# Elementwise work of the mixers moved from GpSimd to VectorE in a two-layer hybrid trunk

## The chip, the cores and the metric

One core of a Trainium2 chip runs the whole program. The metric is device time in microseconds (us): three runs of the kernel before gave 1460.66 to 1461.21 us, median 1460.79 us. The engines are called by the names of the profile: PE (TensorE, matmuls), PEld (its weight loads), DVE (VectorE), ACT (ScalarE), POOL (GpSimd) and SP (SyncE, which only issues DMAs here).

## What is computed

Two layers over 256 tokens of width 1024, all in float32. Each layer is a gated feed-forward block, a mixer of three branches, and a second feed-forward block. The change touches branch a and the rotation of branch c:

```python
u = causal_depthwise_conv(rg_x, conv_w[l], conv_b[l])            # 4 taps
y_a = rg_lru(u, ...) * jax.nn.gelu(rg_g)

def rg_lru(u, w_a, b_a, w_x, b_x, lam):
    r = sigmoid(block_matmul(u, w_a) + b_a)
    i = sigmoid(block_matmul(u, w_x) + b_x)
    log_a = (-RG_C * softplus(-lam)) * r
    a = exp(log_a)
    b = sqrt(-expm1(2.0 * log_a)) * (i * u)
    _, h = associative_scan(combine, (a, b), axis=1)             # h = a*h + b
    return h

def apply_rope(x, cos, sin):
    x1, x2 = split(x, 2, axis=-1)
    return concatenate([x1 * cos - x2 * sin, x2 * cos + x1 * sin], axis=-1)
```

Branch b is a stick-breaking attention, branch c a softmax attention with low-rank queries and keys. The three branches are gated by sigmoids, summed, multiplied by an output matrix and added to x.

## The kernel before

**Matmuls.** float32 values are split in two parts, hi and lo, and a product is made from three of them (hi·hi, hi·lo, lo·hi), so that PE runs at its rate for the fp32r type. The weights come from HBM as one long stream (`raw`, 1 MB a load, issued by SP) and are split on the way in `split_to` (line 414): ACT writes `hi` (a cast of 128x1024), DVE writes `lo` (raw minus hi, 128x1024). Such a 128x1024 stretch is called a piece here. There are 4 buffers each of hi and lo, and the split is made two pieces ahead of the matmul that reads it (`AHEAD`, line 381). A piece feeds 16 matmuls: in `feature_group` (line 511), 8 of 512 columns and 8 of 256.

**Side work.** Everything else is "side work": taking a finished group out of the PSUM banks (`acc`), scaling it, the convolution, the recurrence, the attentions. It is written as Python generators. When the program is built, `Tasks` (line 222) feeds their operations into the stream of matmuls: it keeps a clock for each engine (`Clock`, line 124) that is advanced by fixed costs (`Op`, lines 170 to 190; for DVE 68 + 1.042 ns a column, for POOL 150 + 2.1 ns a column), and `fits` (line 266) lets an operation in when those clocks say that its inputs are there. A small matmul of the side work, which writes a `side` bank, goes in when its inputs will be ready within 60 ns of PE's clock; other work when it starts not later than about 50 ns after that engine's or PE's clock and ends within `LIMIT` (line 227), 1800 ns ahead of PE. The order that comes out is fixed in the program: each engine works through its own list, and waits at an instruction whose inputs are late.

**What the change touches.** `rg_x` (832, with `conv` at 833): u is made of one multiply-add with the bias (line 847, on POOL) and three `scalar_tensor_tensor` on DVE, for each half of 256 columns; its weights `rgw` come by a DMA that POOL issues. `rg_g` (860): gelu by tanh, with the cubic (lines 865 and 866) on POOL. `rg_chain` (879): splits u and its weights in `r` tiles by ACT and DVE, six small matmuls a half into `side`, sigmoids, then the products of lines 910, 925 and 934 on POOL and two scans on DVE. `q_rope` (1062): the rotation of two token tiles (line 1073), one on POOL and one on DVE, six operations each in `rope` (1048). Names in the trace: `f` is any scratch tile of 128x512, `r` a tile of split parts, `rc` the row norms of the two low-rank inputs, `cs` the table of cosines and sines. Nearly every instruction is recorded by one helper and so carries line 201; groups are told apart by their tiles.

What stays on POOL: the sums of squares in `squares` (650), the inverse square roots, one memset in `k_rope`, the `rgw` DMAs, and the last normalisation.

Of the kernel before, what the change touches and what calls it, by code (L numbers as in the profile page):

```python
# [10 lines left out]
AF = mybir.ActivationFunctionType  # L11
ALU = mybir.AluOpType
# [12 lines left out]
V_F1, V_MIX, V_F2, V_CW, V_CB, V_BA, V_BX, V_LAM, V_QN, V_KVN = 0, 8, 16, 24, 56, 64, 72, 80, 88, 90  # L25
# [312 lines left out]
def trunk(tc, xT_in, pos_in, w_in, rgw_in, fin_in, const_in, out):  # L338
# [4 lines left out]
    with ctx:  # L343
# [8 lines left out]
        vec = cst[:, 0:C_FIRST]  # L352
# [19 lines left out]
        act, dve, pe, gp, sp = (  # L372
            Timed(e, n, clock, tasks)
            for e, n in ((nc.scalar, "act"), (nc.vector, "dve"), (nc.tensor, "pe"), (nc.gpsimd, "pool"), (nc.sync, "sp"))
        )
# [456 lines left out]
        def rg_x(mx, p):  # L832
            def conv(f):
                vo = mx["v"]
                w = yield from FT.take()
                gp.dma_start(out=w, in_=rgw_in[mx["l"], :, p * 512:(p + 1) * 512])
                mx["rgw"][p] = w
                u = yield from FT.take()
                for j in range(2):
                    k = p * 2 + j  # L840
                    fs, us = f[:, j * 256:(j + 1) * 256], u[:, j * 256:(j + 1) * 256]

                    def cw(tap):
                        c = vo + V_CW + tap * 8 + k
                        return vec[:, c:c + 1]

                    gp.tensor_scalar(us, fs, cw(3), vec[:, vo + V_CB + k:vo + V_CB + k + 1], op0=ALU.mult, op1=ALU.add)
                    for d in range(1, 4):
                        dve.scalar_tensor_tensor(out=us[:, d:], in0=fs[:, :256 - d], scalar=cw(3 - d), in1=us[:, d:], op0=ALU.mult, op1=ALU.add)
                yield  # L850
                FT.give(f)
                mx["u"][p] = u

            def run(a):
                f = yield from scaled(a, mx["nm"], "rb")
                yield
                tasks.spawn(conv(f))
            return run

        def rg_g(mx, p):  # L860
            def gelu(x):

                t = yield from FT.take()
                act.activation(out=t, in_=x, func=AF.Square)
                gp.tensor_scalar(t, t, 0.044715, 1.0, op0=ALU.mult, op1=ALU.add)
                gp.tensor_tensor(t, t, x, op=ALU.mult)
                act.activation(out=t, in_=t, func=AF.Tanh, scale=0.7978845608028654)
                dve.scalar_tensor_tensor(out=x, in0=t, scalar=1.0, in1=x, op0=ALU.add, op1=ALU.mult)
                yield
                FT.give(t)  # L870
                mx["gT"][p] = x

            def run(a):
                f = yield from scaled(a, mx["nm"], "rb")
                yield
                tasks.spawn(gelu(f))
            return run

        def rg_chain(mx, ps):

            vo = mx["v"]

            for p in ps:
                while p not in mx["u"]:
                    yield 1
                u = mx["u"][p]
                w = mx["rgw"][p]
                wt = yield from RT.take()
                ut = yield from RT.take()
                wr, ur = [x.rearrange("p k c t -> p k (c t)") for x in (wt, ut)]  # L890
                for x, r in ((w, wr), (u, ur)):
                    act.copy(r[:, 0], x)
                    dve.tensor_tensor(r[:, 1], x, r[:, 0].bitcast(F32), op=ALU.subtract)
                A = yield from FT.take()
                I = yield from FT.take()
                T = yield from FT.take()
                for j in range(2):
                    k = 2 * p + j
                    s = slice(j * 256, (j + 1) * 256)
                    b = yield from side.take()  # L900
                    for q in range(2):
                        c = slice((j * 2 + q) * 128, (j * 2 + q + 1) * 128)
                        for x, (i, d) in enumerate(((0, 0), (0, 1), (1, 0))):
                            pe.matmul(b[:, q * 256:(q + 1) * 256], wr[:, i, c], ur[:, d, s], start=x == q == 0, stop=x == 2, skip_group_check=True)
                    for q, (dst, vb) in enumerate(((A, V_BA), (I, V_BX))):
                        act.activation(out=dst[:, s], in_=b[:, q * 256:(q + 1) * 256], func=AF.Sigmoid, bias=vec[:, vo + vb + k:vo + vb + k + 1])
                    yield
                    side.give(b)
                    act.activation(out=T[:, s], in_=A[:, s], func=AF.Tanh, scale=s4[:, mx["l"], k:k + 1], bias=tiny)
                gp.tensor_tensor(I, I, u, op=ALU.mult)  # L910
                yield
                FT.give(w, u)
                RT.give(wt, ut)
                mx["rgw"].pop(p)
                mx["u"].pop(p)
                mx["tanh"] += 1
                while mx["tanh"] < p // 2 * 2 + 2:
                    yield 1
                for j in range(2):
                    s = slice(j * 256, (j + 1) * 256)  # L920
                    act.activation(out=A[:, s], in_=A[:, s], func=AF.Exp, scale=m8[:, mx["l"], 2 * p + j:2 * p + j + 1])
                act.activation(out=T, in_=T, func=AF.Ln)
                act.activation(out=T, in_=T, func=AF.Exp, scale=0.5)
                dve.scalar_tensor_tensor(out=I, in0=A, scalar=1.0, in1=I, op0=ALU.add, op1=ALU.mult)
                gp.tensor_tensor(I, I, T, op=ALU.mult)
                for j in range(2):
                    s = slice(j * 256, (j + 1) * 256)
                    dve.tensor_tensor_scan(T[:, s], A[:, s], I[:, s], 0.0, op0=ALU.mult, op1=ALU.add)
                yield
                FT.give(A, I)  # L930
                while p not in mx["gT"]:
                    yield 1
                g = mx["gT"].pop(p)
                gp.tensor_tensor(g, g, T, op=ALU.mult)
                hl = yield from RT.take()
                hilo(g, hl, g=0.5)
                yield
                FT.give(g, T)
                mx["ya"][p] = hl
# [108 lines left out]
        def rope(e, dst, src, tmp, nh, t):  # L1048

            co = cs[:, 0, t:t + 1].to_broadcast([128, nh, 32])  # L1050
            si = cs[:, 1, t:t + 1].to_broadcast([128, nh, 32])
            e.tensor_tensor(tmp[:, :, 0:32], src[:, :, 32:64], si, op=ALU.mult)
            e.tensor_tensor(tmp[:, :, 32:64], src[:, :, 0:32], si, op=ALU.mult)
            e.tensor_tensor(dst[:, :, 0:32], src[:, :, 0:32], co, op=ALU.mult)
            e.tensor_tensor(dst[:, :, 32:64], src[:, :, 32:64], co, op=ALU.mult)
            e.tensor_tensor(dst[:, :, 0:32], dst[:, :, 0:32], tmp[:, :, 0:32], op=ALU.subtract)
            e.tensor_tensor(dst[:, :, 32:64], dst[:, :, 32:64], tmp[:, :, 32:64], op=ALU.add)

        def split_heads(ap, nh):
            return ap.rearrange("p (h d) -> p h d", h=nh)  # L1060

        def q_rope(mx):
            def run(a):
                qs = yield from gen_scaled(a, mx["rq"])
                yield
                tasks.spawn(rest(qs))

            def rest(qs):
                ro = []
                for t in range(NT):  # L1070
                    f = yield from FT.take()
                    tmp = yield from FT.take()
                    rope((gp, dve)[t], split_heads(f, 8), split_heads(qs[t], 8), split_heads(tmp, 8), 8, t)
                    yield
                    FT.give(tmp)
                    ro.append(f)
                    yield
                FT.give(*qs)
                yield
                for p in range(2):  # L1080
                    b = yield from transpose_pair(ro, p * 256)
                    f = yield from FT.take()
                    act.copy(f, b)
                    yield
                    side.give(b)
                    mx["qr"][p] = f
                FT.give(*ro)
            return run
# [429 lines left out]
```

## Time and profile before

| | us |
|---|---|
| median of 3 runs | 1460.79 |
| the profiled execution | 1463.23 |
| its span, first to last instruction | 1461.4 |
| PE busy | 1442.5 |
| PEld busy | 1261.0 |
| DVE busy | 1108.8 |
| ACT busy | 888.8 |
| POOL busy | 144.5 |

The profiled execution takes 1.8 us more than its span and lies 2.4 us above the median. Mean granted clock of PE: 0.998 of full speed. The mixer of layer 0 runs from about 200 to 552 us of the span, that of layer 1 from about 920 to 1273; the stretches between are the feed-forward blocks. The moved operations stand in the two mixers alone, and alike in both, so what is said of one layer counts twice.

### The profile page before, as it was taken

What the parts mean: (1) busy time and instruction counts of PE and PEld (TensorE: products, weight loads), DVE (VectorE), ACT (ScalarE), POOL (GpSimd) and SP (SyncE); (2) the same over time, 40 slices, a digit from 0 to 9 for tenths busy, and PEclk for the clock granted to TensorE, in tenths of its full rate; (3) what the DMA queues carried; (4) which work ended last, traced back from release to release, by engine and by line L of the source; (5) the groups of instructions that cost most, each with busy time, mean ns of one, the idle gap of its engine ahead of it and who ended that gap; (6) DMA issues with size and microseconds to landing.
All of it is one profiled execution on the core that took longest, in us unless ns stands there. A gap on an engine that the chain in (4) does not pass through costs nothing.

```text
span 1461.4 us, 20833 instructions
## 1 busy us (share of the span) xinstructions
PE 1442.5 (99%) x8276; PEld 1261.0 (86%) x8276; DVE 1108.8 (76%) x1548; ACT 888.8 (61%) x1365; POOL 144.5 (10%) x118
## 2 busy tenths in 40 slices
PE   8999999999999999999999999999999999999998
PEld 7888889888888888888888888898888888888886
DVE  5887567689987788876677776676989877877853
ACT  4665446888665556555455554479885656566543
POOL 2000001123410000000000000111323000100001
PEclk9999999999999999999999999999999999999999
DMA  6555554444543455455545455544444434545452
GB/s 244 201 185 192 200 179 163 170 151 147 197 148 145 171 179 194 179 200 178 198 173 201 177 198 184 200 159 155 141 171 174 173 138 166 199 175 201 176 199 87
DMA packets 37506, 258.17 MB, mean 177 GB/s; under 512 B 4256, under 2 KB 4640, under 8 KB 6816
## 3 DMA queue, kind: packets, MB, share of 16 engines
q1 hardware_dynamic: 35856, 253.16, 48.0%
q0 software_dynamic: 832, 2.62, 0.6%
q8 instruction: 65, 1.06, 0.3%
q10 hardware_dynamic: 720, 1.05, 0.2%
q14 instruction: 33, 0.27, 0.1%
HBM read 255.77 MB, written 1.05 MB: 176 GB/s over the span
## 4 chain that ended last, share of the span: by engine, by line
PE 90%; DVE 7%; issue 1%; ACT 1%; DMA 0%; ACTq 0%; POOLq 0%; POOL 0%; DVEq 0%
PE acc L201 76%; PE side L201 14%; DVE f L201 3%; DVE lo L201 3%; DVE r L201 1%; DMA x<-xT 0%; ACT f L201 0%; ACT hi L201 0%; ACT r L201 0%; ACTq L396 0%; POOLq L1514 0%; POOL rms L201 0%; DVE rms L201 0%; DVEq L201 0%
## 5 line engine op out<-in xcount | busy, mean ns | idle before, releaser
L201 PE MATMUL acc<-r,hi 128*128 128x512 f32 x3116 | 1000.3, 402 | 0.0
L201 DVE TENSOR_TENSOR lo<-raw,hi 128x1024 fp32r<-128x1024 f32 (+1 forms) x478 | 591.4, 1239 | 231.4 <-ACT hi L201 230.2
L201 PEld LDWEIGHTS acc<-r,lo 128*128 128x128 f32 x3116 | 585.2, 188 | 137.7
L201 PE MATMUL acc<-r,lo 128*128 128x256 f32 x3116 | 613.4, 278 | 0.0
L201 ACT CAST hi<-raw 128x1024 fp32r<-128x1024 f32 (+1 forms) x478 | 496.9, 1045 | 128.8 <-PE acc L201 91.9
L201 PEld LDWEIGHTS acc<-r,hi 128*128 128x128 f32 x3116 | 481.5, 189 | 5.0
L201 POOL TENSOR_TENSOR f<-f,f 128x512 f32<-128x512 f32 (+1 forms) x51 | 90.9, 1787 | 1043.3 <-ACT f L201 959.9
L201 ACT COPY f<-acc 128x512 f32<-128x512 f32 x164 | 96.0, 585 | 121.4 <-PE acc L201 121.2
L201 ACT ACTIVATE f<-f 128x256 f32<-128x256 f32 (+3 forms) x190 | 94.9, 502 | 85.6 <-DVE f L201 84.4
L201 DVE TENSOR_TENSOR f<-acc,f 128x512 f32<-128x512 f32 x166 | 113.9, 686 | 41.6 <-ACT f L201 41.2
L201 DVE TENSOR_TENSOR f<-f,f 128x512 f32<-128x512 f32 (+1 forms) x177 | 125.0, 706 | 7.8 <-ACT f L201 1.6
L201 ACT CAST r<-f 128x256 fp32r<-128x256 f32 (+2 forms) x130 | 58.7, 456 | 63.4 <-DVE f L201 59.7
L201 PE MATMUL acc<-hi,r 128*128 128x512 f32 (+2 forms) x344 | 96.9, 358 | 0.0
L201 PE MATMUL side<-r,hi 128*128 128x512 f32 x260 | 84.5, 396 | 0.0
L201 PE MATMUL side<-f,f 128*128 128x256 f32 (+1 forms) x320 | 71.7, 328 | 0.0
L201 PEld LDWEIGHTS acc<-hi,r 128*128 128x128 f32 x344 | 61.6, 189 | 8.3
L201 DVE TENSOR_TENSOR r<-f,r 128x256 fp32r<-128x256 f32 (+2 forms) x130 | 64.7, 502 | 1.9 <-ACT r L201 1.9
L201 PE MATMUL acc<-lo,r 128*128 128x512 f32 (+2 forms) x172 | 61.0, 355 | 0.0
L201 PE MATMUL side<-r,lo 128*128 128x256 f32 x260 | 60.5, 279 | 0.0
L201 PEld LDWEIGHTS side<-r,hi 128*128 128x128 f32 x260 | 45.6, 188 | 7.5
L201 PEld LDWEIGHTS side<-r,lo 128*128 128x128 f32 x260 | 47.0, 188 | 4.0
L201 PEld LDWEIGHTS side<-f,f 128*128 128x128 f32 x320 | 46.0, 191 | 0.5
(95 smaller groups left out, 839.1 us busy)
## 6 DMA issues: line engine op xcount, KB each, us to landing
raw<-w SPq DMA_DIRECT2D x239, 1024.0 KB, 4.8
f<-rgw POOLq DMA_DIRECT2D x8, 256.0 KB, 3.6
raw<-w SPq DMA_DIRECT2D x4, 256.0 KB, 5.7
out<-f SPq DMA_DIRECT2D x4, 256.0 KB, 2.2
x<-xT ACTq DMA_DIRECT2D x3, 256.0 KB, 6.9
f<-fin POOLq DMA_DIRECT2D x2, 256.0 KB, 3.4
cst<-const SPq DMA_DIRECT2D x1, 336.0 KB, 8.3
x<-xT ACTq DMA_DIRECT2D x2, 128.0 KB, 3.8
```

Of the source, the lines that this page charges most:

```text
L201: return self.f(*self.args, **self.kw)
```

## The change

Four places name DVE where they named POOL, and the cubic of gelu becomes one instruction: instead of t = 0.044715·x² + 1 and t·x it computes (x² + 1/0.044715)·x, and the tanh that follows takes the factor 0.044715 into its scale.

```diff
-                    gp.tensor_scalar(us, fs, cw(3), vec[:, vo + V_CB + k:vo + V_CB + k + 1], op0=ALU.mult, op1=ALU.add)
+                    dve.tensor_scalar(us, fs, cw(3), vec[:, vo + V_CB + k:vo + V_CB + k + 1], op0=ALU.mult, op1=ALU.add)
...
                 act.activation(out=t, in_=x, func=AF.Square)
-                gp.tensor_scalar(t, t, 0.044715, 1.0, op0=ALU.mult, op1=ALU.add)
-                gp.tensor_tensor(t, t, x, op=ALU.mult)
-                act.activation(out=t, in_=t, func=AF.Tanh, scale=0.7978845608028654)
+                dve.scalar_tensor_tensor(out=t, in0=t, scalar=1.0 / 0.044715, in1=x, op0=ALU.add, op1=ALU.mult)
+                act.activation(out=t, in_=t, func=AF.Tanh, scale=0.7978845608028654 * 0.044715)
...
-                gp.tensor_tensor(I, I, u, op=ALU.mult)
+                dve.tensor_tensor(I, I, u, op=ALU.mult)
...
-                gp.tensor_tensor(I, I, T, op=ALU.mult)
+                dve.tensor_tensor(I, I, T, op=ALU.mult)
...
-                gp.tensor_tensor(g, g, T, op=ALU.mult)
+                dve.tensor_tensor(g, g, T, op=ALU.mult)
...
-                    rope((gp, dve)[t], split_heads(f, 8), split_heads(qs[t], 8), split_heads(tmp, 8), 8, t)
+                    rope(dve, split_heads(f, 8), split_heads(qs[t], 8), split_heads(tmp, 8), 8, t)
```

Because the costs of these operations in the builder's clocks change with the engine, the order of all side work in the mixers comes out anew. In all, DVE's list gains 60 instructions, POOL's loses 68, and ACT's loads of function tables go from 33 to 29. Three places, each in the mixer of layer 0:

The first is on DVE, at the convolution of the first pair of blocks (`f_117` holds its input, `f_119` its output, `lo` is a piece of the weight stream, `acc` a finished group); the first number of a tile's name tells tiles apart.

```order
 L201 TENSOR_TENSOR f_117<-f_117,f_108 128x512
-L201 TENSOR_TENSOR lo<-raw,hi 128x1024
+L201 TENSOR_SCALAR f_119<-f_117,cst 128x256
 L201 SCALAR_TENSOR_TENSOR f_119<-f_117,cst,f_119 128x255
 L201 SCALAR_TENSOR_TENSOR f_119<-f_117,cst,f_119 128x254
+L201 TENSOR_TENSOR lo<-raw,hi 128x1024
 L201 SCALAR_TENSOR_TENSOR f_119<-f_117,cst,f_119 128x253
+L201 TENSOR_SCALAR f_119<-f_117,cst 128x256
+L201 SCALAR_TENSOR_TENSOR f_119<-f_117,cst,f_119 128x255
```

The convolution's first step stands in DVE's list now, its second half starts at once behind the first, and a piece of weights is split later by two instructions of the convolution.

The second is on DVE, where it is most crowded. Before, around the last convolution and the splits of the recurrence's operands into `r` tiles (a `SCALAR_TENSOR_TENSOR` that writes 256 columns from two `f` tiles is a scan):

```order
L201 TENSOR_TENSOR r_100<-f_133,r_100 128x384
L201 SCALAR_TENSOR_TENSOR f_122<-f_111,cst,f_122 128x253
L201 TENSOR_TENSOR lo<-raw,hi 128x1024
L201 TENSOR_TENSOR f_123<-acc_84,f_123 128x512
L201 TENSOR_TENSOR f_123<-f_123,f_108 128x512
L201 SCALAR_TENSOR_TENSOR f_132<-f_130,f_131 128x256
L201 TENSOR_TENSOR r_98<-f_120,r_98 128x512
L201 TENSOR_TENSOR lo<-raw,hi 128x1024
L201 TENSOR_TENSOR r_103<-f_121,r_103 128x512
L201 TENSOR_TENSOR r_93<-f_122,r_93 128x512
```

And with the change, the longest run of DVE work between two pieces of weights:

```order
L201 TENSOR_TENSOR f_129<-f_129,f_128 128x512
L201 SCALAR_TENSOR_TENSOR f_128<-f_125,f_129 128x256
L201 TENSOR_TENSOR lo<-raw,hi 128x1024
L201 SCALAR_TENSOR_TENSOR f_128<-f_125,f_129 128x256
L201 SCALAR_TENSOR_TENSOR f_120<-f_113,cst,f_120 128x253
L201 TENSOR_SCALAR f_120<-f_113,cst 128x256
L201 SCALAR_TENSOR_TENSOR f_120<-f_113,cst,f_120 128x255
L201 SCALAR_TENSOR_TENSOR f_120<-f_113,cst,f_120 128x254
L201 SCALAR_TENSOR_TENSOR f_120<-f_113,cst,f_120 128x253
L201 TENSOR_TENSOR r_99<-side_86,r_99 128x2x256
L201 TENSOR_TENSOR r_94<-f_117,r_94 128x512
L201 TENSOR_TENSOR lo<-raw,hi 128x1024
```

Between two pieces of weights DVE had at most four other instructions in the rows before; now eight stand there, among them a moved one (`TENSOR_SCALAR`), and a moved product (`f_129<-f_129,f_128`) stands ahead of the scan that reads it.

The third is POOL's list in the same mixer. Before, one stretch of it read:

```order
L201 TENSOR_SCALAR f_109<-f_109 128x512
L201 TENSOR_TENSOR f_109<-f_109,f_124 128x512
L201 TENSOR_SCALAR f_113<-f_113 128x512
L201 TENSOR_TENSOR f_113<-f_113,f_110 128x512
L201 TENSOR_SCALAR f_136<-f_136 128x512
L201 TENSOR_TENSOR f_136<-f_136,f_123 128x512
```

Now the whole mixer's list up to its sums of squares is:

```order
L201 DMA f_118<-rgw 128x512
L201 DMA f_121<-rgw 128x512
L201 TENSOR_SCALAR rc_1791<-ssc_1790 128x2
L201 TENSOR_TENSOR rc_1791<-rc_1791,nhalf 128x2
L201 DMA f_117<-rgw 128x512
L201 DMA f_111<-rgw 128x512
L201 TENSOR_SCALAR rc_1791<-ssc_1790 128x2
L201 TENSOR_TENSOR rc_1791<-rc_1791,nhalf 128x2
L201 MEMSET f_128 128x512
```

POOL keeps the weight loads of the recurrence, two inverse square roots and a memset, with nothing of 512 columns that reads tiles between them.

## Rows read from the trace of the kernel before

**Rows 1.** The page: busy time of each engine over the whole span.

```profile
PE 1442.5 (99%) x8276; PEld 1261.0 (86%) x8276; DVE 1108.8 (76%) x1548; ACT 888.8 (61%) x1365; POOL 144.5 (10%) x118
```

**Rows 2.** Waits of PE in the whole span: us in total, times, longest.

```profile
PE side L201 <- DVE r L201: 4.7, 4, 1.5
...
PE side L201 <- DVE f L201: 2.4, 4, 1.0
```

**Rows 3.** Waits of PE's weight loads on DVE, whole span.

```profile
PEld side L201 <- DVE r L201: 5.5, 4, 1.7
PEld side L201 <- DVE f L201: 3.3, 4, 1.2
```

**Rows 4.** Mixer 0 by stretches: us; PE, PEld, DVE, ACT, POOL busy; PEclk; DMA; GB/s.

```profile
320.00:340.00 20.00, 17.97 (x109) 15.71 (x107) 19.93 (x23) 16.89 (x27) 11.28 (x8) 1.00 0.33 116
340.00:360.00 20.00, 19.69 (x118) 17.46 (x119) 17.62 (x21) 16.79 (x32) 6.93 (x4) 1.00 0.40 149
380.00:400.00 20.00, 19.84 (x124) 18.07 (x123) 19.51 (x26) 9.07 (x17) 6.41 (x5) 1.00 0.51 167
400.00:420.00 20.00, 18.96 (x112) 16.52 (x111) 19.01 (x36) 13.87 (x22) 5.73 (x4) 1.00 0.53 184
420.00:440.00 20.00, 20.00 (x118) 17.53 (x117) 16.13 (x30) 11.33 (x27) 0.00 (x0) 1.00 0.40 142
```

**Rows 5.** Timeline, DVE, 318 to 344 us: start, us, instruction; first of these undisturbed.

```profile
318.07 0.69 DVE L201 TENSOR_TENSOR f<-f,f 128x512 f32<-128x512 f32 x1
318.68 0.68 DVE L201 TENSOR_TENSOR_SCAN f<-f,f 128x256 f32<-128x256 f32 x1
...
328.85 0.48 DVE L201 SCALAR_TENSOR_TENSOR f<-f,cst,f 128x254 f32<-128x254 f32 x1
329.24 1.22 DVE L201 TENSOR_TENSOR lo<-raw,hi 128x1024 fp32r<-128x1024 f32 x1
...
331.27 1.51 DVE L201 SCALAR_TENSOR_TENSOR f<-f,cst,f 128x253 f32<-128x253 f32 x1
...
337.89 2.36 DVE L201 TENSOR_TENSOR r<-f,r 128x512 fp32r<-128x512 f32 x2
340.18 0.68 DVE L201 TENSOR_TENSOR r<-side,r 128x512 fp32r<-128x512 f32 x1
...
341.98 2.31 DVE L201 TENSOR_TENSOR lo<-raw,hi 128x1024 fp32r<-128x1024 f32 x1
```

**Rows 6.** Timeline, POOL, same stretch; idle before in brackets.

```profile
331.02 1.47 POOL L201 TENSOR_TENSOR f<-f,f 128x512 f32<-128x512 f32 x1
...
336.98 2.13 POOL L201 TENSOR_TENSOR f<-f,f 128x512 f32<-128x512 f32 x1
341.53 5.63 POOL L201 TENSOR_TENSOR f<-f,f 128x512 f32<-128x512 f32 x3 [2.43 <-DVE f L201]
```

**Rows 7.** Timeline, DVE, mixer 0: beside moved POOL work, the first, one between, the last.

```profile
229.49 1.18 DVE L201 SCALAR_TENSOR_TENSOR f<-f,cst,f 128x255 f32<-128x255 f32 x2
...
401.82 1.85 DVE L201 TENSOR_SCALAR f<-cst,rc 128x128 f32<-128x128 f32 x2
...
417.15 1.33 DVE L201 TENSOR_TENSOR f<-f,f 128x512 f32<-128x512 f32 x1
```

**Rows 8.** Groups by form: count, busy us, mean ns of one, idle before.

```profile
L201 DVE TENSOR_SCALAR f<-f,sm 128x256 f32<-128x256 f32 x16 | 5.5, 346 | 0.0
L201 DVE TENSOR_TENSOR f<-f,cs 128x256 f32<-128x256 f32 x8 | 3.3, 410 | 0.0
L201 DVE TENSOR_SCALAR f<-acc,rms 128x512 f32<-128x512 f32 x4 | 3.0, 745 | 0.0
L201 DVE TENSOR_TENSOR f<-f,f 128x256 f32<-128x256 f32 x8 | 3.4, 421 | 0.1
L136 ACT ACT_TABLE_LOAD x33 | 42.3, 1283 | 5.1 <-DMA x<-xT 4.6
```

**Rows 9.** The chain that ended last, a stretch of the first feed-forward block.

```profile
23.75 159.19 PE acc L201 x912
```

## The prediction

> **What bounds the kernel now.** I read the page first: PE is busy 1442.5 of 1461.4 us, DVE 1108.8, POOL 144.5 [rows 1]. Only what PE waits for can be won. The list of PE's waits comes next [rows 2]. The start of the program aside, which the change does not touch, it holds PE, before a small product of the side work, waiting for DVE, and nothing else: 4.7 us in 4 waits on an `r` tile and 2.4 us in 4 waits on an `f` tile, together **7.1 us**, half in each mixer. There is no row for `lo`: the weight pieces were never late. The weight loads' own waits at these same places come to 5.5 + 3.3 = 8.8 us [rows 3], because a weight load that was held starts its pipeline anew. The stretches [rows 4] say where the waits lie: PE misses 2.0, 0.3, 0.2 and 1.0 us in the 20 us from 320, 340, 380 and 400, the stretches where POOL works most (5.7 to 11.3 us of 20) and DVE is full (17.6 to 19.9); from 420, without POOL, it misses nothing. The granted clock is 1.00 in all of them, so no term below is the clock's.
>
> Then I ask why DVE is late there. The timeline of DVE [rows 5] has the same forms both alone and beside POOL: a product of 512 columns takes 0.69 us, a convolution step 0.48, a piece of weights 1.22; but a step at 331.27 takes 1.51, a piece at 341.98 takes 2.31, and two splits into `r` at 337.89, that take about 0.68 each elsewhere, take 2.36 together. At those moments POOL is in a product [rows 6]: 331.02 to 332.49, 336.98 to 339.11, 341.53 to 347.16. The split at 337.89 is what PE waits 1.5 us for. In mixer 0 there are 23 DVE instructions that overlap a moved POOL instruction and take over 0.1 us more than their form takes alone, from the second of the two steps at 229.49 to the product at 417.15 (1.33 against 0.69 us) [rows 7]; I sum their surplus to 14.6 us, 29.2 us over both layers.
>
> **The change, part by part.**
>
> *Added to DVE, per layer:* 8 first steps of the convolution, 256 columns, at 0.35 us (the nearest row is the scaling by `sm`, 346 ns) = 2.8 us; 4 cubics at 0.69 = 2.8; 12 products at 0.69 = 8.3 [rows 5, 8]; the rotation, 4 operations at 0.41 and 2 at 0.42 [rows 8] = 2.5. Sum 16.4 us a layer, 32.7 us in all. The first step is the only form without a row of its own; between 0.35 and the 0.48 of a later step, the eight differ by 1 us. DVE's instructions overlap a little: the scan at 318.68 starts 0.61 us after a product of 0.69 us [rows 5], so 60 instructions occupy 32.7 - 60 x 0.08 = 27.9 us.
>
> *Taken from DVE:* the surplus of 29.2 us, since of POOL's work in the mixers only two inverse square roots, the loads of `rgw`, a memset and the sums of squares remain. Bounds: all of it, or, if the surplus came from elsewhere than POOL, nothing. Rows 5 to 7 put it at the upper end. **So DVE's load is the same to within 4 us:** it gains instructions and loses their disturbance.
>
> *PE:* its list holds the same matmuls in another order, 99% busy; cost nothing. *ACT:* four table loads fewer, 4 x 1.28 = 5.1 us [rows 8], won beside other work; the change of scale is free. *POOL's queue:* the four `rgw` loads a layer stood behind products and now stand behind nothing, so they come earlier; the square roots too. Neither was on the path. The wait of about 1 us at 402 us was for the tile that spreads the row norms over the columns: DVE made it in two steps of 128 columns that took 1.85 us together beside a product of POOL [rows 7], though 256 columns of that kind take 0.35 alone [rows 8].
>
> *What PE then waits for.* The 7.1 us go: each was a DVE instruction lengthened by POOL's, or standing behind one. Bounds: 8.8 us if the restart of the weight loads goes too, 0 if the moved load takes up the room. What is late next is a split into `r` or an `f` tile that now stands behind a moved instruction: the order was made with 601 ns for a product that takes 690. I put one such delay of 0.7 us in each layer, 1.4 us. Bounds for new waits: 0 (from 420 us on there is none, [rows 4]) to the 12.4 us of the second rival. Sum on the profiled execution: 1463.2 - 7.1 + 1.4 = 1457.5; it lies 2.4 us above the median, so on the median 1460.8 - 5.7 = **1455.1 us**, 0.39% less. A measurement of this kernel can tell about 0.2%, 2.9 us, from no change.
>
> **A rule weighed.** The trace shows a piece of weights going from 1.22 to 2.31 us beside POOL [rows 5]. The Trainium skill, "SBUF — State Buffer", section "Who interferes with whom", says that an instruction of VectorE with two SBUF inputs contends with one of GpSimd that reads SBUF, and that the loser blocks. The trace agrees with contention; how long the blocking lasts is taken from the rows. Against the change speaks the Trainium skill, "Perfetto Trace Analysis", section "Optimizing Scalar/DVE Operations": with VectorE saturated, moving work off it, even to GpSimd, may make sense. By that the sum would be the third case below; the same section adds that the two share a read port, so that such a move might not help, and with this the rows agree.
>
> **Rivals.**
>
> *1. The waits are only exchanged.* DVE was full from 320 to 340 us (19.93 of 20) and would stay full with the load that replaces the surplus; PE would wait for other splits. For: the equal load; the disturbance in 320 to 340 us is about what the moved instructions there would cost. Against: the builder's clocks knew nothing of the disturbance and placed the small products too early; the moved load they do know. Time: 1460.8, 1458 to 1463.7.
>
> *2. DVE's list becomes the bound, slower.* The change makes a stretch between two pieces with eight other instructions, at the scans of the first pairs. Over its two pieces DVE has, before the first, one evacuation 0.75 [rows 8], a product and a fused one 0.69 each, a split 0.68, a step 0.48 and a scan 0.68, then the piece 1.22, then a scan 0.68, four steps 1.9, a first step 0.35, two splits 1.36 and a piece 1.22: 10.7 us, less 15 overlaps of 0.08, 9.5 us. PE spends 159.19/912 = 0.175 us a matmul [rows 9], 5.6 us on two pieces, and about 0.7 us on six products of `r` between. DVE falls 3.1 us behind. Pieces are split two ahead, 5.6 us, so this costs nothing while DVE comes in with over 3.1 us in hand, and up to 3.1 us each time when it comes in with none, say after waiting at the head of its list for ACT (a table load is 1.28 us). Products and cubics that wait for ACT now hold up the pieces queued behind them, which they did not on POOL. At two such places a layer it is 12.4 us: 1460.8 - 7.1 + 12.4 = 1466.1. It decides from 3.5 us of new waits a layer on. Against: before, with DVE at 19.93 of 20, no piece was late [rows 2, 4].
>
> *3. More is won.* If the 8.8 us go entire, with no new waits, 1452.0.
>
> That the change doesn't do what it says is excluded: the 60 instructions stand in DVE's list, and POOL's is short of 68.
>
> **How the numbers follow.** Forecast, 1452.9 to 1457.8: 0.55. Rival 1: 0.25. Rival 2: 0.15. Rival 3: 0.05. I let the range run from 1451.5, just under rival 3, to 1464.5, above rival 1 and a mild form of rival 2, which leaves out some 0.13. The forecast's own range, 1452.9 to 1457.8, stands beside it. Faster by over 2.9 us (under 1457.9): forecast and rival 3, 0.60. Within 2.9 us: rival 1 and a little of the mild form, 0.26. Slower: 0.14.
>
> **What would show it.** POOL's busy time falls to under half of 144.5 us. DVE's stays at 1109 us within 10; the form `lo` in the mixers goes back to 1.22 us, and DVE rows over twice their form's time are left only at the sums of squares. The four waits of PE on `r` and `f` in rows 2 become under 2 us in all. Wrong would be: waits of PE on `lo`, or waits on `r` that come to 7 us again (rival 1), or DVE busy time of 1135 us or more, which says that the surplus wasn't POOL's.

## The result and the profile after

| | us |
|---|---|
| changed kernel, median of 4 runs (lowest, highest) | 1475.38 (1475.03, 1475.75) |
| kernel before, 4 runs beside them | 1461.00 (1460.66, 1462.22) |
| ratio, 95% interval | 1.0097 (1.0079 to 1.0114) |
| its profiled execution, and span | 1475.33, 1473.6 |

The change makes the kernel 14.4 us slower. The forecast was 1455.1, faster, and the range ended at 1464.5: both are wrong. I compare the two profiled executions by their spans, 1473.6 against 1461.4: 12.2 us more. Both begin alike: a wait of PE on `f` of 2.7 us before and 2.6 us now, and behind it 3.4 us at about half of the granted clock (0.54 and 0.50 from 10.5 to 13.9 us). Some profiled executions further below begin without half clock; in that of the last experiment, whose matmuls come in the same order up to 410 us, PE is 2.3 to 2.6 us earlier from 14 us on. So spans can be compared only where the start is the same.

The busy line of the page, to be read against [rows 1]:

```profile
PE 1450.1 (98%) x8276; PEld 1266.4 (86%) x8276; DVE 1112.6 (76%) x1608; ACT 884.8 (60%) x1361; POOL 42.8 (3%) x50
```

DVE has 60 instructions more and only 3.8 us more to do, and POOL has lost 101.7 us. That part went as forecast, and the groups by form say why. Their columns are count, busy us, mean ns of one, and idle before:

```profile
L201 DVE TENSOR_TENSOR lo<-raw,hi 128x1024 fp32r<-128x1024 f32 x474 | 577.8, 1221 | 223.4 <-ACT hi L201 222.5
...
L201 DVE TENSOR_SCALAR f<-f,cst 128x256 f32<-128x256 f32 x16 | 6.5, 409 | 0.2
```

A piece of weights is back at 1.22 us, its undisturbed length in [rows 5], and the convolution's first step, the form without a row before, takes 0.41 us.

PE, with the same 8276 matmuls, is busy 7.6 us longer. That is the first thing that no step of the prediction allows for. The waits of PE over the whole span (us in total, times, longest), to be read against [rows 2], are:

```profile
PE acc L201 <- DVE r L201: 7.7, 4, 2.4
PE side L201 <- DVE r L201: 2.8, 2, 1.4
PE acc L201 <- DVE f L201: 2.6, 1, 2.6
PE acc L201 <- DMA raw<-w: 1.2, 1, 1.2
PE side L201 <- ACT r L201: 1.0, 2, 0.5
PE side L1351 <- DVE tiny L1368: 1.0, 1, 1.0
```

The third, the fourth and the last lie at the start of the program. Half of the other three lies in each mixer: 11.5 us where there were 7.1. The longest is a new kind: a matmul of the *main* stream, into `acc`, waits for a split into `r`. No wait on `lo` is there.

Stretches of the changed kernel in mixer 0 (length; PE, PEld, DVE, ACT, POOL busy; granted clock; DMA; GB/s):

```profile
320.00:340.00 20.00, 20.00 (x120) 17.73 (x119) 16.00 (x24) 16.78 (x25) 0.00 (x0) 1.00 0.39 137
340.00:344.00 4.00, 2.06 (x12) 1.53 (x10) 3.92 (x7) 1.42 (x4) 0.00 (x0) 1.00 0.85 309
...
440.00:444.00 4.00, 2.58 (x15) 1.85 (x14) 3.63 (x8) 2.28 (x4) 0.00 (x0) 1.00 0.31 129
444.00:448.00 4.00, 1.55 (x8) 1.41 (x8) 3.55 (x7) 2.30 (x6) 0.00 (x0) 0.92 0.02 4
```

From 320 to 340 us, where PE missed 2.0 us in [rows 4], it now misses nothing: those waits, of branch a's small products, went as forecast. But it misses 1.9 us from 340 to 344 us, before two products of branch b (they read `tri_r`), and 3.9 us from 440 to 448. In the kernel before, PE missed nothing in the second place:

```profile
440.00:444.00 4.00, 4.00 (x26) 3.51 (x26) 3.55 (x10) 2.49 (x5) 0.00 (x0) 1.00 0.46 180
444.00:448.00 4.00, 4.00 (x27) 3.64 (x26) 2.73 (x6) 2.74 (x4) 0.00 (x0) 1.00 0.66 256
```

The same view shows what lengthened PE's busy time. In four stretches of 3.4 us, two in each mixer, where the kernel before has 1.00, the granted clock is 0.50, which is 1.2 instead of 2.4 GHz:

```profile
345.00:348.40 3.40, 3.40 (x13) 2.96 (x12) 0.69 (x1) 1.66 (x3) 0.00 (x0) 0.50 0.00 0
447.40:450.80 3.40, 3.40 (x14) 2.94 (x12) 0.67 (x2) 0.79 (x2) 0.00 (x0) 0.50 0.50 169
1072.00:1075.40 3.40, 3.40 (x12) 3.03 (x13) 1.00 (x2) 1.87 (x3) 0.00 (x0) 0.50 0.00 0
1174.40:1177.80 3.40, 3.40 (x12) 2.86 (x11) 0.94 (x2) 1.31 (x2) 0.00 (x0) 0.50 0.57 183
```

PE is full in each of them and does half of what it could: 1.7 us lost, 6.8 us in four. So of the 12.2 us, 11.5 - 7.1 = 4.4 are waits and 6.8 the clock; about 1 us I haven't traced.

Why does PE wait at 441 us? In the timeline of PE and DVE there (start, us, instruction, in brackets the idle time before and what ended it) DVE makes the two last splits, and PE uses them at once:

```profile
440.05 0.69 DVE L201 SCALAR_TENSOR_TENSOR f<-f,f 128x512 f32<-128x512 f32 x1
440.83 0.69 DVE L201 SCALAR_TENSOR_TENSOR r<-f,r 128x512 fp32r<-128x512 f32 x1
441.57 0.73 PE L201 MATMUL acc<-r,hi 128*128 128x512 f32 x2 [1.42 <-DVE r L201]
...
444.35 0.69 DVE L201 TENSOR_TENSOR f<-f,f 128x512 f32<-128x512 f32 x1
...
445.74 0.69 DVE L201 SCALAR_TENSOR_TENSOR r<-f,r 128x512 fp32r<-128x512 f32 x1
446.49 0.73 PE L201 MATMUL acc<-r,hi 128*128 128x512 f32 x2 [2.44 <-DVE r L201]
...
448.14 1.41 PE L201 MATMUL acc<-r,hi 128*128 128x512 f32 x2
```

These `r` tiles are the recurrence's results: `rg_chain` ends with a split of its product with the gate, one for each of four pairs of 128-row blocks, and branch a's output matmul, the next group of the main stream, reads the four in turn. The product at 444.35 is the moved one of line 934. The last row shows the half clock: two matmuls that took 0.73 us at 446.49 take 1.41.

Matching the program's list of each engine to its trace, instruction by instruction, gives for each pair in mixer 0 when its split ended and when PE first read it (us of the span):

| kernel | pair 1 | pair 2 | pair 3 | pair 4 |
|---|---|---|---|---|
| before | 348.9, 441.0 | 379.3, 442.4 | 412.3, 444.2 | 420.2, 446.6 |
| changed | 356.8, 435.1 | 368.6, 437.4 | **441.5, 441.6** | **446.4, 446.5** |

The last two pairs had 32 and 26 us in hand and now have none. DVE isn't slow at this place: with the disturbance gone every form has its quiet length. The program's *order* puts these splits late. The builder's own clocks, too, hold a wait of 2.4 us before pair 3 and one of 2.3 us before pair 4, and in the kernel before none there. That is **theory 1**: the builder made another order for DVE's and PE's lists, and this order is what costs. **Theory 2**: DVE carries the moved load at its full length, so any order would be late. **Theory 3**, which goes with either: the waits cost little, and the clock behind them doubles the price.

### The profile page after: what moved, and what is told of

It is laid out like the page before. It is cut to its first block, busy times and chain, and to the rows that moved or that the text cites. A ratio compares the mean times of both kernels' runs of the same rounds, so it can differ in the third digit from the quotient of the medians.

```text
span 1473.6 us, 20787 instructions
## 1 busy us (share of the span) xinstructions
PE 1450.1 (98%) x8276; PEld 1266.4 (86%) x8276; DVE 1112.6 (76%) x1608; ACT 884.8 (60%) x1361; POOL 42.8 (3%) x50
## 4 chain that ended last, share of the span: by engine, by line
PE 93%; DVE 3%; ACT 1%; issue 1%; DMA 0%; ACTq 0%; POOLq 0%; POOL 0%
PE acc L201 79%; PE side L201 15%; DVE f L201 2%; DVE lo L201 1%; ACT hi L201 1%; ACT f L201 1%; DMA x<-xT 0%; DVE r L201 0%; ACT r L201 0%; DVE sm L201 0%; ACT L136 0%; ACTq L396 0%; POOLq L1513 0%; POOL rms L201 0%; DVE rms L201 0%
## 5 line engine op out<-in xcount | busy, mean ns | idle before, releaser
L201 DVE TENSOR_TENSOR lo<-raw,hi 128x1024 fp32r<-128x1024 f32 (+1 forms) x478 | 580.3, 1216 | 223.4 <-ACT hi L201 222.5
L201 PEld LDWEIGHTS acc<-r,hi 128*128 128x128 f32 x3116 | 481.4, 189 | 14.1 <-DVE r L201 9.3
L201 DVE TENSOR_TENSOR f<-f,f 128x512 f32<-128x512 f32 (+1 forms) x205 | 138.1, 675 | 8.3 <-ACT f L201 2.1
L201 PE MATMUL side<-f,f 128*128 128x256 f32 (+1 forms) x320 | 75.9, 343 | 0.0
L201 DVE TENSOR_TENSOR r<-f,r 128x256 fp32r<-128x256 f32 (+2 forms) x130 | 61.5, 479 | 1.9 <-ACT r L201 1.9
L201 POOL TENSOR_TENSOR f<-f,f 128x512 f32<-128x512 f32 x15 | 24.3, 1621 | 948.2 <-ACT f L201 948.1
```

Source lines behind the costliest of these rows:

```text
L201: return self.f(*self.args, **self.kw)
```

## The experiments

### The order of before, with the change

All moved work runs on DVE, but the builder counts it as POOL's, with POOL's costs and clock, and the cubic is left as two steps. So the order is that of before.

```diff
+        gpd = Timed(nc.vector, "pool", clock, tasks)
...
-                dve.tensor_tensor(I, I, u, op=ALU.mult)
+                gpd.tensor_tensor(I, I, u, op=ALU.mult)
```

and so at the other moved places.

> All six pieces run on VectorE, but the builder's clocks count them as GpSimd work with GpSimd's cost, so every other instruction stands in the order of the kernel before (gelu's cubic keeps its two steps). If the time was lost to the order that the builder made of the dearer VectorE (theory 1), the waits of PE on branch a's r tiles are gone, the granted clock never falls in the mixers, and the time is 1453 to 1458 us, as first forecast. If the work itself is too much for VectorE (theory 2), PE waits somewhere for it whatever the order, and the time is 1470 us or more.

Measured: 1460.46 us (1459.95 to 1462.41), ratio to before 0.9997 (0.9988 to 1.0006). PE's waits:

```profile
PE side L201 <- DVE r L201: 5.0, 4, 1.5
...
PE side L201 <- DVE f L201: 1.3, 2, 0.6
...
```

Nothing is lost, so theory 2 falls: the same operations on the same engine cost nothing in the old order. But nothing is won either, and the 1453 to 1458 us of theory 1 are not reached. PE's list is that of the kernel before, matmul by matmul, so each wait of mixer 0 can be followed. The two on `r`, of 0.88 us at 336.5 and 1.46 us at 340.3, became none and 1.03; the one on `f` of 1.04 us at 403.7 went, while one of 0.16 at 395.2 grew to 0.63. And one of 1.47 us is new, before a product of branch b:

```profile
331.50 0.44 PE L201 MATMUL side<-r,tri_r 128*128 128x384 f32 x1 [1.47 <-DVE r L201]
338.95 0.62 PE L201 MATMUL side<-r,r 128*128 128x256 f32 x3 [1.03 <-DVE r L201]
```

No POOL product is there to disturb DVE, but DVE is as full as before, busy 19.61 of the 20 us from 320. The waits are exchanged for others of nearly the same sum, 6.3 us for 7.1, which is rival 1. The order of the changed kernel thus costs 1475.4 - 1460.5 = 14.9 us, more than the whole loss.

### The order of the changed kernel, with the work on GpSimd

The mirror image: the builder counts the work as DVE's, and POOL executes it (the cubic in two instructions).

```diff
+        pld = Timed(nc.gpsimd, "dve", clock, tasks)
...
-                dve.tensor_tensor(I, I, u, op=ALU.mult)
+                pld.tensor_tensor(I, I, u, op=ALU.mult)
```

> The reverse: the six pieces run on GpSimd as before (the cubic in two steps), but the builder counts them as VectorE work, so the order is the changed kernel's. Theory 1: the waits on branch a's r tiles and the two falls of the clock per layer are there all the same, and the contention comes on top: 1475 to 1485 us. Theory 2: VectorE is relieved again, 1459 to 1465 us.

Measured: 1478.65 us (1477.50 to 1478.85), ratio 1.0117 (1.0103 to 1.0131). PE's waits:

```profile
PE acc L201 <- DVE r L201: 9.1, 4, 3.8
PE side L201 <- DVE r L201: 4.0, 2, 2.0
...
PE side L201 <- ACT r L201: 1.0, 2, 0.5
...
```

The loss is there with POOL doing the work: the order carries it on either engine. PE waits before the same matmuls as in the changed kernel, in sum somewhat longer (14.1 us for 11.5), and the granted clock falls at the same places (0.67 from 344 to 348 us, 0.60 from 448 to 452).

### Matmuls that fill the wait

In the changed kernel, 20 and 36 small matmuls on constant data, whose results nobody reads, are put ahead of pairs 3 and 4 of branch a, so that PE works where it waited. They only add work.

```diff
+                    if self.fill and p in self.fill and side.free:
+                        w = side.now()
+                        for _ in range(self.fill[p]):
+                            nc.tensor.matmul(w[:, 0:128], warm, warm, start=True, stop=True)
+                        side.give(w)
                     yield from kts_of([self.src[p]])
...
```

> The changed kernel with 20 and 36 small extra matmuls (128 columns, bf16, result unused) ahead of the two matmul groups of the first branch-a group that wait for the third and fourth pair. PE's wait becomes work of about the same length. If half of the clock's cost comes from the fall at 447 us (and 1174 us), that fall goes and 2 x 1.7 = 3.4 us come back: 1471 to 1473 us. If the clock's fall is not tied to these waits, it stays at 1475 us or grows by what the extra matmuls overrun.

Measured: 1469.99 us (1467.00 to 1470.84), ratio 1.0057 (1.0043 to 1.0071): 5.4 us better than the changed kernel, by added work alone. The profiled execution took 1467.0 us; its stretches:

```profile
340.00:344.00 4.00, 2.58 (x13) 2.04 (x14) 1.74 (x3) 0.80 (x2) 0.00 (x0) 1.00 0.56 233
344.00:348.00 4.00, 4.00 (x27) 3.56 (x26) 3.03 (x4) 3.88 (x6) 0.00 (x0) 1.00 0.00 0
...
448.00:452.00 4.00, 4.00 (x27) 3.52 (x26) 3.30 (x11) 1.52 (x6) 0.00 (x0) 1.00 0.13 53
```

The clock no longer falls behind 446 us, as theory 3 says, nor at the same place in the other mixer. In this execution it doesn't fall at 345 us either, where nothing was changed and PE waits just as long, nor at the start of the program, where PE is busy 17.58 of the first 20 us instead of 15.26. So the 8.3 us by which this execution is shorter than the profiled one of the changed kernel are not all the filling's: the two falls that it was made for are 3.4 of them. The five executions lie from 1467.0 us at a mean granted clock of 0.999 to 1470.8 at 0.997, so one of the other falls seems to come in some of them; only one was profiled, and I leave that open.

### Wider limits in the builder

The changed kernel, with two settings by which the builder admits an operation of DVE or ACT: it may end 2400 instead of 1800 ns ahead of PE and start 150 instead of 50 ns late. No operation changes, only the order.

```diff
-    LIMIT = 1800
-    SLACK = 50
+    LIMIT = 2400
+    SLACK = 150
```

> The changed kernel with two of the builder's settings widened: side work may end 2400 instead of 1800 ns ahead of PE, and start 150 instead of 50 ns after it. Same work on the same engines, another order, in which branch a's pairs come earlier. Theory 1: the waits at branch a go, 1453 to 1460 us. Theory 2: 1470 us or more, as the load on VectorE is the same.

Measured: **1453.91 us** (1453.46 to 1455.56), ratio to before 0.9951 (0.9938 to 0.9965): faster than both kernels. The busy line of its page, and all waits of PE that it has:

```profile
PE 1441.7 (99%) x8276; PEld 1261.0 (87%) x8276; DVE 1110.9 (77%) x1608; ACT 882.5 (61%) x1361; POOL 44.7 (3%) x50
```

```profile
PE acc L201 <- DMA raw<-w: 1.1, 1, 1.1
PE side L1351 <- DVE tiny L1368: 1.0, 1, 1.0
PE acc L201 <- DVE f L201: 0.8, 2, 0.6
```

The three are the start of the program; in the mixers PE waits for nothing, and its busy time is back at that of [rows 1]. Pairs 3 and 4 are split at 404.0 and 422.1 us and first read at 432.3 and 433.8. The gain over before, 1461.0 - 1453.9 = 7.1 us, is the sum of PE's waits in [rows 2]: the price of the forecast's main term was right, and it needed an order in which the splits come in time.

### Controls of that gain

**The same settings on the kernel before** (the diff is the same two lines).

> The kernel before with the two widened settings alone (2400 and 150 ns), all pieces on GpSimd. If the settings by themselves make a better order, it is 1453 to 1456 us, as the run with the change and the same settings was. If that run had a good order by chance of its costs, this one has another, in which PE waits for small products of the mixers, 1462 to 1475 us.

Measured: 1478.85 us (1478.50 to 1480.42), ratio 1.0114 (1.0099 to 1.0129). PE's waits in this kernel:

```profile
PE side L201 <- DVE f L201: 8.0, 4, 2.5
PE acc L201 <- DVE f L201: 7.0, 8, 2.3
...
```

So the settings bring nothing of themselves; here they make some 16 us of waits in the mixers, one of 0.8 us on `lo` among them, and the clock falls once in each mixer. The time is above what I expected. A setting's worth depends on the work it orders.

**The order of the 1453.9 us kernel, with the work on GpSimd**: that kernel's list, and the edit of the second experiment.

> The order of the run with the widened settings (1453.9 us, PE waited for nothing in the mixers), but the six pieces run on GpSimd. Only the contention is added, some 29 us of longer VectorE instructions. If most of it hides behind PE, 1455 to 1461 us with a few waits of PE on r or f tiles; if VectorE's lateness goes to PE in full, 1470 us or more; if contention costs nothing there, 1453 to 1454.5 us.

Measured: 1462.48 us (1461.94 to 1464.38), ratio 1.0005 (0.9996 to 1.0015), between the first and the second case above. PE's waits:

```profile
PE side L201 <- DVE f L201: 4.1, 4, 1.6
PE acc L201 <- DVE f L201: 2.3, 2, 2.1
PE side L201 <- ACT hi L201: 1.6, 2, 0.8
...
```

The second is the start of the program. In one and the same order of work, then, moving it from GpSimd to VectorE is worth 1.0005 - 0.9951 = 0.54%, 7.9 us. The trace shows, in the mixers, 5.7 us of waits, one half-clock stretch behind waits of 1.6 and 0.5 us that end at 406.0 and 406.9 us and, for a product on DVE of 512 columns, a mean of 719 ns where DVE has the work alone 692. The Trainium skill, "Perfetto Trace Analysis", section "Optimizing Scalar/DVE Operations", warns that moving work between these two engines might not help, since they share a read port. In this case having the work on GpSimd costs 7.9 us in this order, nothing in that of before (0.9997), and 0.2%, within the intervals, in that of the changed kernel (1.0117 against 1.0097).

### Admission alone

The builder asks of an operation on DVE whether it starts and ends in time (`fits`); one on POOL is always let in. In this variant of the changed kernel the moved operations count on DVE's clock, but are always let in, as they were on POOL.

```diff
-        if op.e in ("pool", "sp"):
+        if op.e in ("pool", "sp") or op.free:
             return True
...
```

> The changed kernel, but the builder lets the moved instructions in without its test, as it does for GpSimd's; they are counted on VectorE's clock with their cost. If that test is what held branch a's chain back, the third and fourth pair are split 10 us or more ahead of their first matmul, and the two waits there are gone; other waits may come, so the time can lie anywhere from 1456 to 1478 us. If the cost on VectorE's clock alone is what held it back, both pairs still end just as PE needs them, and it stays near 1475 us.

Measured: 1464.03 us (1461.91 to 1467.17), ratio 1.0015 (1.0004 to 1.0025). Pairs 3 and 4 are split at 409.0 and 427.1 us and read at 443.5 and 444.9, early again, and 11.4 us of the loss are gone. So the admission of the moved operations is what held the chain back. What is left are waits at other places, on `r` in the main stream among them:

```profile
PE acc L201 <- DVE r L201: 5.9, 4, 2.0
PE side L201 <- DVE f L201: 2.3, 2, 1.1
...
```

What joins these places stands in the builder. It has two ways past `fits`: where the main stream comes to a tile that isn't there yet, `drain` (line 317) puts the missing operations into the lists at once, and where it lacks a `side` bank, `wait` (line 308) does so after a few rounds. Following the building of the kernels shows which operations are forced in like this. All have one such place at the end of each mixer, without a wait of PE. Besides it the changed kernel has two in each mixer: a split and products with `tri_r` of branch b, and the last splits of pairs 3 and 4, which `fits` never let in. These are the places where PE waits. The order of before and that of the changed kernel with the wide limits have none. This variant has three in each mixer, and PE's three waits of mixer 0, which end at 364.6, 374.8 and 500.4 us, stand at these three. Not every wait has this cause: the kernel before with the wide limits has no such place either, and its PE waits the most.

The variant also shows how uneven the clock's part is. The wait that ends at 500.4 us has its like at 1223.1 us in the other mixer, both 1.99 us long, and the stretches about 1 us behind them read:

```profile
501.40:504.80 3.40, 3.40 (x12) 2.87 (x12) 1.63 (x4) 1.53 (x2) 0.00 (x0) 0.51 0.67 282
1224.00:1227.40 3.40, 3.40 (x22) 2.96 (x21) 2.03 (x4) 1.53 (x2) 0.00 (x0) 1.00 0.68 282
```

Over its ten executions the time goes from 1461.9 us at a mean granted clock of 0.998 to 1467.2 at 0.995.

### The rotation alone

Only the rotation moves; convolution, cubic and products stay on GpSimd.

```diff
-                    rope((gp, dve)[t], split_heads(f, 8), split_heads(qs[t], 8), split_heads(tmp, 8), 8, t)
+                    rope(dve, split_heads(f, 8), split_heads(qs[t], 8), split_heads(tmp, 8), 8, t)
```

> Only the rotation is moved to VectorE; everything else as in the kernel before. The order changes only after the rotation's place, and branch a's chain is untouched. If the loss comes from branch a's late pairs, this run is within 0.2% of the kernel before, 1458 to 1463 us; if the moved load as such costs, a part in proportion (2.5 of 16.4 us a layer) shows: about 2 us more.

Measured: 1459.46 us (1459.15 to 1461.85), ratio 0.9987 (0.9977 to 0.9996). PE's waits:

```profile
PE side L201 <- DVE r L201: 4.7, 4, 1.5
...
PE side L201 <- DVE f L201: 0.8, 2, 0.4
```

The waits on `f` of [rows 2] shrink from 2.4 to 0.8 us, which is most of the 2.1 us gained over the kernel before beside it, and the waits on `r` stay, before the same matmuls. The wait that went is the one of 1.04 us at 403.7. Up to 410 us the lists of PE, DVE and ACT are those of the kernel before, and in mixer 0 POOL's differs only by the rotation, six instructions from 374.9 to 382.3 us, which is missing. Three instructions of DVE beside it took 1.23, 1.76 and 1.21 us, now 0.68, 1.22 and 0.69. The two steps to which the prediction had put the wait down still take as long, beside a product that stays on POOL:

```profile
397.60 1.84 DVE L201 TENSOR_SCALAR f<-cst,rc 128x128 f32<-128x128 f32 x2
```

So lateness that DVE had gathered 20 us earlier was enough to make that wait. This part of the change is harmless. Which of the other parts throws the order, one by one, I didn't run.

## Why the prediction was wrong

- **The step that failed** is the one on PE: "its list holds the same matmuls in another order, 99% busy; cost nothing". The order wasn't free: 14.9 us lie between the changed kernel and the same work in the old order. I had looked at the new order on DVE and POOL around the convolutions and scans, and not at where PE reads what the moved chain ends in. There the builder forces a split in directly before its reader, which was to be seen before any run, as were the 2.4 and 2.3 us in the builder's own clocks.
- **New waits** were put at 1.4 us, a split late by 0.7 us in each layer. The waits were 11.5 us. Of these, 7.7 were for the last splits of the recurrence, which end 26 to 29 us later than before and were forced in; 3.8 were for splits before branch b's products with `tri_r`, forced in likewise. The upper bound of 12.4 us held for the waits alone.
- **"No term below is the clock's"** was read from a kernel in which the mixers ran at 1.00 throughout, and carried over to another order. The four falls cost 6.8 us, more than the 4.4 us by which the waits grew.
- **"The 7.1 us go"** held for most of the single waits, but in the old order others came in their place (first experiment: 6.3 us in all), since DVE stayed as full: that is rival 1, and the forecast fails there even without the new order. It held in the order with wide limits, and gave just that sum. That such an order came out was no part of the forecast.
- **The wait at 402 us** was put down to the two steps beside a product of POOL. They are part of it at most: it went in the last experiment with these steps as long as before, when DVE was no longer held up at the rotation.
- **DVE's load** was right: 1112.6 us where 1109 within 10 was forecast, `lo` at 1.22, POOL under half. The convolution's first step is 0.41 us and not 0.35, 0.9 us in sixteen.
- **The slower rival** had the right sign, by the wrong place: it put pieces of weights late behind products that wait for ACT, 12.4 us. No wait on `lo` came, though the long stretch between two pieces is there.

Shown: the order costs, on either engine; PE waits where the builder forces operations in, the late pairs above all; the admission of the moved operations makes these late; the clock's falls take more than the waits grew. Open: why the wide limits suit the work on DVE and not that on GpSimd, which of the moved parts throws the order, and what decides whether a wait is followed by a fall.

## What to carry to other kernels

Where a scheduler lays out the program from cost tables, moving an operation to another engine is a new schedule first and a new cost second: read the new order at the *end* of the moved chain, where the bounding engine consumes it, and compare how far ahead each producer stands. Where the scheduler can force an operation past its own test, list the forced ones: here every kernel has one such place in a mixer that costs nothing, and in the two kernels that have more, each further one was a wait. To price the move itself, hold the order fixed and change only the engine; here that took one line, and it separated 14.9 us of order from the 0 to 7.9 us that the engine was worth. A result that is lost to the order may be won back by the scheduler's own settings, but they are to be tried together with the change, since on the kernel before the same settings lost 1.1%.

## What the runs showed of the hardware

- Short waits of a busy PE can be followed by half clock. Waits of 0.5 and 1.4 us that ended at 342.1 and 344.0 us, with PE busy 2.06 of 4 us, came before one fall, waits of 1.4 and 2.4 us before the other; each fall lasts 3.4 us and takes 1.7. Yet the kernel with filling matmuls had 0.5 and 1.4 us at the first place and no fall in the execution profiled, and the first experiment had four waits on `r`, the longest 1.5 us, and none. Even within one execution like waits differ: 1.99 us in both mixers of the seventh experiment, with a fall in the first alone.
- GpSimd's disturbance of VectorE, 29 us summed over instructions in the kernel before, was worth nothing, 0.2% or 7.9 us of the kernel's time on three fixed orders of work. Where it cost 7.9 us, it stood as 5.7 us of waits of PE and one fall of the clock; I take it that only the part ahead of something that PE waits for counts, which no run shows in general. That part can lie far ahead: without the rotation on GpSimd, three instructions of VectorE at 378 to 383 us lost 1.6 us, and a wait of PE of 1.04 us at 403.7 was gone.
